# Two more groups of seven products, four groups of query blocks, and rotation tables made once: a change to one inference step of a hybrid decoder layer

## The chip, the cores and the metric

The kernel runs on one core of one Trainium2 chip. The metric is the device time of one execution in microseconds (us), lower is better. Before the change the three timed runs took 1263.16, 1267.95 and 1266.23 us, a median of 1266.23 us.

In the text, PE is the engine for matrix products, PEld its weight loads, DVE the vector engine, ACT the scalar engine, POOL the general engine and SP the engine whose queue issues most of the transfers. L1382 is line 1382 of the kernel before.

## The reference

One layer reads 536 tokens (16 meta tokens, 512 prompt tokens, 8 sample tokens) of width 2048, all float32. One wide product `x @ w_in` feeds two branches, sliding-window attention and a complex diagonal state space (S5), which are gated and merged:

```python
h = jnp.einsum('btd,de->bte', rmsnorm(x, norm_gain), w_in)
q, k, v, z_a, u, z_s, g_a, g_s = jnp.split(h, IN_SPLITS, axis=-1)   # 1024, 256, 256, 1024, 1024, 1024, 2048, 2048 wide
q, k = rope(rmsnorm(q, q_gain), pos), rope(rmsnorm(k, k_gain), pos)
o_attn = sink_attention(q, k, v, window 128, 16 meta keys)
lam_bar = jnp.exp(lam * dt)                                         # 64 groups x 64 complex states
h_t = lam_bar * h_{t-1} + b_bar @ u_t;  y = gelu(Re(c @ h_t) + d * u)
y = y * sigmoid(y @ w_glu + b_glu)
out = x + (sigmoid(g_a) * ((o_attn * silu(z_a)) @ w_attn_out) + sigmoid(g_s) * ((y * silu(z_s)) @ w_ssm_out)) @ w_out
```

The outputs are the new tokens, the key and value windows and the states.

## The kernel before

**Products.** Every weight and every activation is split into a high and a low part, and each product of 128x128 weights with 260 columns (half of the tokens) is three matmuls: high by high, low by high, high by low. A block is 128 output columns for all tokens; over the 2048 inputs it takes 16 x 3 x 2 = 96 matmuls (`mm`, L1157, the matmul itself L1168). The splits are made while the weights stream in (`Stream.piece`, L1004): a transfer on SP's queue, a cast on ACT (L1008), a subtraction on DVE (L1009), two units of 128x1024 for a block.

**Groups.** `Quads` (L1026) and `quad` (L1386) compute two blocks together by a scheme of the Strassen kind: seven products (`product`, L1379, matmul L1382) of 8 x 3 = 24 matmuls in place of eight. Each group needs four raw units, some of them summed on DVE (L1073), seven casts on ACT (L1074) and seven subtractions on DVE (L1075); the weights are made three products ahead (`get(ahead=3)`, L1083). The activations' sums (`tau`) are made beforehand.

**Order of the work.** The 48 gate blocks ("x"), 8 state space inputs ("u") and 12 heads' blocks ("h": 2 of keys, 2 of values, 8 of queries) come in this order: five x blocks while the input is loaded; NA = 4 x blocks; NQ = 15 groups of two x blocks (L1511); then the list ORDER1 (L946), "x" and then u and h in turn, the last five h in a row; then x blocks until all are made (L1676). The GLU's eight half blocks (Y1), the state space's output product (Y2, 16 half blocks, L1719), the attention's output product (A, L1737) and eight groups for `w_out` (L1771) end the kernel.

**Background.** All other work lies in three lanes of generators (`Background`, L952). After every two or four weight tiles of a block (`GRAIN`) and after every product of a group, `bg.step` adds a budget to a credit (at most `cap` is carried over) and runs generator steps until the credit is spent. Each step yields its cost, by the author's own count in us of DVE; `None` ends a lane's turn. With `fair` set the lanes take turns, otherwise the first lane goes first. Lane 0 holds the state space's preparation (`ssm_prep`), the eight state space sets (`ssm(n)`, begun by each u block) and then `attention()`; lane 1 the sets' constants (`ssm_consts`); lane 2 the decoding samples (`samples`).

This order is only where the code writes the work down. A scheduler then orders each engine's queue by its own plan: weights and evacuations have a high priority, and an instruction may be put ahead of its place in the text when the plan finds its inputs ready and its engine free. `issue_after(ins)` (called `later()` in the generators) puts instructions behind `ins` on the engine of `ins`; `bg.last` is a matmul. An engine works through its queue in order and waits at each instruction for its inputs.

**The state space's preparation** (L149) is a chain of some 200 small POOL instructions on 128x32 to 128x704 elements, in the time of the groups. It makes the powers of the rotation, T6 and T11, last (L272 and L275), and a transposed factor (L287). Its result goes to DRAM (L1499) and is read back when the list ORDER1 begins. In each of the eight sets `ssm_consts` builds the rotation table of 66 steps from T6 and T11 with six DVE instructions (L404 to L421). `ssm_block` (L444) multiplies the inputs by the table (L483, L484), scans two stretches of 66 (L503), rotates back (L509 to L513) and forms the outputs.

**The heads.** `heads(i)` (L1325) multiplies a block by the tokens' norm (L1331) into a tile of the name "z", writes it to DRAM twice, the second time with halves exchanged (five transfers on SP's queue), squares it on ACT, and, after each second block, sums the squares by a small matmul (`sums`, L1349). After the last h block `head_norms` (L1361) loads the sums and takes reciprocal roots by a chain of twelve small DVE instructions, first for the keys (rkD), then for the queries (rqD), in four tiles of the name "z", of which there are two buffers. An x block's evacuation (`evac`, L1198) needs such a tile too; a u block's goes to `uf` (L1581). `attention()` (L1587) begins when `normed` is set behind it: it loads keys, values and queries, rotates them (`rope`, L707, with the roots from rkD and rqD), and goes through four key groups. `samples()` begins at the same place. `attended()` (L1658) splits the attention's result for the product A at the end; `bg.drain()` (L1727) puts down whatever background is left before A.

Of the kernel before, what the change touches and what calls it, by code (L numbers as in the profile page):

```python
# [67 lines left out]
def cmul(v, pool, out, a, br, bi, sh, tag):  # L68
# [14 lines left out]
        ("T6", (2, 32, 6)), ("T11", (2, 32, 11)), ("car", (2, 32)))  # L83
NKEPT = sum(int(np.prod(s)) for _, s in KEPT)
# [53 lines left out]
def kept(ap):  # L138

    r, o = {}, 0  # L140
    for nm, sh in KEPT:
# [7 lines left out]
def ssm_prep(nc, K, tmp, psum, dram, R, ident, a_prm, later):  # L149
# [18 lines left out]
    yield 3.0  # L168
# [6 lines left out]
    yield 3.0  # L175
# [33 lines left out]
    yield 3.0  # L209
# [19 lines left out]
    yield 2.5  # L229
# [15 lines left out]
    def powers(tab, z, cnt, tag):  # L245
# [9 lines left out]
        for zp in zs:  # L255
# [6 lines left out]
            yield 1.5  # L262
        norm(tab, (32, cnt), "nt")
        yield 2.0
# [19 lines left out]
    yield 1.0  # L284
    for _ in range(8):
        yield None
# [12 lines left out]
    yield 0.0  # L299

# [22 lines left out]
def ssm_consts(nc, pool, dram, R, D, ub, a_bT, a_bN, a_cT, e32, d_skip, later, free):  # L323
# [41 lines left out]
    nc.sync.dma_start(out=B, in_=a_bT[ub])  # L365
    CL = pool.tile([P, 4, 2, 5, 32], F32, name="CL")
# [37 lines left out]
    tab = pool.tile([P, 2, 4, L], F32, name="tab")  # L404
    x = R["T11"][:, :, ps]
    y = R["T6"][:, :, ps]
    t1 = pool.tile([P, 4, 11, 6], F32, name="rt1", bufs=1)
    t2 = pool.tile([P, 4, 11, 6], F32, name="rt2", bufs=1)
    tv = tab.rearrange("p r a (i j) -> p r a i j", j=6)

    def outer(dst, i, j):
        v.tensor_tensor(out=dst, in0=bc(x[:, i], 3, 6), in1=bc(y[:, j], 2, 11), op=ALU.mult)
    outer(t1, 0, 0)
    outer(t2, 1, 1)
    v.tensor_tensor(out=tv[:, 0].rearrange("p a i j -> p (a i j)"), in0=t1.rearrange("p a i j -> p (a i j)"),
                    in1=t2.rearrange("p a i j -> p (a i j)"), op=ALU.subtract)
    outer(t1, 0, 1)
    outer(t2, 1, 0)
    v.scalar_tensor_tensor(out=tv[:, 1].rearrange("p a i j -> p (a i j)"), in0=t1.rearrange("p a i j -> p (a i j)"),
                           scalar=-1.0, in1=t2.rearrange("p a i j -> p (a i j)"), op0=ALU.mult, op1=ALU.subtract)  # L420
# [6 lines left out]
    yield 2.4  # L427
# [16 lines left out]
def ssm_block(nc, pool, R, D, ub, y_out, later):  # L444
# [27 lines left out]
    yield None  # L472
    for h in range(2):
        p1 = pool.tile([P, 2, 2, NB, L], F32, name="p1", tag="rt1", bufs=1)
        p2 = pool.tile([P, 2, 2, NB, L], F32, name="p2", tag="rt2", bufs=1)
        for i in range(2):
# [3 lines left out]
            for es, b in parts:  # L480
                a = slice(2 * h + es.start, 2 * h + es.stop)
                bi = b[:, :, 0:NC].rearrange("p e (n l) -> p e n l", l=L)
                v.tensor_tensor(out=p1[:, i, es], in0=bi, in1=bc(tab[:, 0, a], 2, NB), op=ALU.mult)  # L483
                v.tensor_tensor(out=p2[:, i, es], in0=bi, in1=bc(tab[:, 1, a], 2, NB), op=ALU.mult)  # L484
                g = slice(4 * ub + a.start, 4 * ub + a.stop)
                v.tensor_tensor(out=R["sst"][:, g, i], in0=R["A0"][:, g, i], in1=b[:, :, NC:140], op=ALU.add)
        wv = w[:, :, 2 * h:2 * h + 2].rearrange("p n a r l -> p r a n l")
        v.tensor_tensor(out=wv[:, 0], in0=p1[:, 0], in1=p2[:, 1], op=ALU.subtract)
        v.tensor_tensor(out=wv[:, 1], in0=p1[:, 1], in1=p2[:, 0], op=ALU.add)
        yield 3.0  # L490
    tre, tim = bc(tab[:, 0], 2, 2), bc(tab[:, 1], 2, 2)
# [14 lines left out]
    for n in range(NB):  # L506
        t1 = pool.tile([P, 4, 2, L], F32, name="rt1", bufs=1)
        t2 = pool.tile([P, 4, 2, L], F32, name="rt2", bufs=1)
        v.tensor_tensor(out=t1, in0=w[:, n], in1=tre, op=ALU.mult)  # L509
        v.tensor_tensor(out=t2, in0=w[:, n], in1=tim, op=ALU.mult)  # L510
        hs = slice(9 + n * L, 9 + n * L + L)
        v.tensor_tensor(out=H[:, :, 0, hs], in0=t1[:, :, 0], in1=t2[:, :, 1], op=ALU.add)
# [576 lines left out]
def trunk(tc, A, O):  # L1089
# [235 lines left out]
    def heads(i):  # L1325
# [16 lines left out]
        def sums():  # L1342
            if "ax" not in S:
                S["ax"] = aux.tile([P, 2, 512], F32, name="aux")
# [605 lines left out]
```

## Time and profile before

| | |
|---|---|
| timed runs, median (lowest to highest) | 1266.23 us (1263.16 to 1267.95) |
| span of the profiled execution, first to last instruction (the page gives no other time of it) | 1262.3 us |
| mean granted clock of PE | 0.997 |
| instructions | 26,537 |
| beginning, five x blocks among it | 0 to about 42 us |
| x blocks one by one (with two of the five) | to 116.1 us |
| fifteen groups | 116.1 to 420.1 us |
| list ORDER1 and x blocks | 420.1 to 828 us |
| GLU and state space's output product | 828 to 1003.8 us |
| attention's output product | 1003.8 to 1096 us |
| groups of `w_out` | 1096 to 1262.3 us |

The profile's page lists each engine's busy time, then the span in 40 slices; a slice is about 31.6 us. Views of the trace give the busy time in chosen stretches, the instructions in order of time, groups of equal instructions, and who waited for whom. "[2.94 <-DVE t L563]" behind an instruction says that its engine stood idle for 2.94 us before it, and which instruction released it by the profile's inference. Matmul durations overlap, since they are pipelined; the distance from one start to the next is what a matmul takes of the span.

### The profile page before, as it was taken

To read this page: it belongs to the slowest core of one execution; us is meant where nothing else is said; L and a number is where in the kernel's file an instruction comes from. 1 tells how busy PE (TensorE), PEld (TensorE's weight loads), DVE (VectorE), ACT (ScalarE), POOL (GpSimd) and SP (SyncE) were. 2 spreads that over 40 slices of the span, in tenths; PEclk is the share of its full clock that TensorE was granted. 3 is DMA by queue.
4 is the path that set the end of the run, shared out by engine and by line. 5 is a ranking of instruction groups with operands and counts; after the bars stand their busy time and mean duration, and the time that the engine had idled before them with its cause. 6 is when DMAs were issued, how large, how long until landed. Compare 5 with 4: busy or idle time off the path is not lost.

```text
span 1262.3 us, 26537 instructions
## 1 busy us (share of the span) xinstructions
PE 1250.9 (99%) x10357; PEld 1227.7 (97%) x10357; DVE 980.6 (78%) x1554; ACT 628.7 (50%) x1344; POOL 266.1 (21%) x437
## 2 busy tenths in 40 slices
PE   9999999999999999999999999999999999999998
PEld 9999999999999999999999999999999999999998
DVE  8687878887778668888897377899887577887875
ACT  8554445444545586556432235567555333344342
POOL 0003999940000033122220123211011000000000
PEclk9999999999999999999999989999999999999999
DMA  8544343443434656555554775777666756555441
GB/s 294 199 160 153 134 143 110 143 150 134 151 126 146 214 172 182 159 165 167 156 159 121 246 211 182 224 240 225 189 214 203 258 174 189 165 192 163 145 139 51
DMA packets 108001, 219.22 MB, mean 174 GB/s; under 512 B 21932, under 2 KB 47492, under 8 KB 107844
## 3 DMA queue, kind: packets, MB, share of 16 engines
q1 hardware_dynamic: 99172, 198.53, 48.5%
q0 software_dynamic: 8704, 19.00, 5.6%
q8 instruction: 81, 1.33, 0.4%
q14 instruction: 44, 0.36, 0.1%
HBM read 181.57 MB, written 36.82 MB: 173 GB/s over the span
## 4 chain that ended last, share of the span: by engine, by line
PE 92%; DVE 3%; DMA 2%; ACT 1%; SPq 1%; issue 0%; DVEq 0%; ACTq 0%
PE mm L1168 45%; PE pr L1382 35%; PE wg L854 2%; PE mm L1255 2%; PE aux L1382 1%; PE aux L1168 1%; PE aux L1255 1%; DVE wlo L1009 1%; PE aux L806 1%; PE aux L805 1%; ACT ct L346 1%; PE tr L526 1%; PE tr L836 1%; PE wg L526 1%; DMA Y<-yD 0%
## 5 line engine op out<-in xcount | busy, mean ns | idle before, releaser
L1075 DVE TENSOR_TENSOR wlo<-raw,whi 128x1024 fp32r<-128x1024 f32 x161 | 198.5, 1253 | 69.6 <-ACT whi L1074 69.0
L1074 ACT CAST whi<-raw 128x1024 fp32r<-128x1024 f32 x161 | 166.4, 1049 | 167.2 <-DVE raw L1073 80.0
L1168 PE MATMUL mm<-xh,whi 128*128 128x260 f32 (+1 forms) x792 | 185.8, 288 | 3.1 <-DVE t L563 2.9
L1008 ACT CAST whi<-raw 128x1024 fp32r<-128x1024 f32 (+3 forms) x128 | 122.3, 965 | 132.3 <-PE mm L1168 85.6
L1168 PE MATMUL mm<-xh,wlo 128*128 128x260 f32 (+1 forms) x792 | 184.4, 287 | 0.0
L1168 PE MATMUL mm<-xl,whi 128*128 128x260 f32 (+1 forms) x792 | 184.1, 286 | 0.0
L1009 DVE TENSOR_TENSOR wlo<-raw,whi 128x1024 fp32r<-128x1024 f32 (+3 forms) x128 | 142.2, 1119 | 46.5 <-ACT whi L1008 45.7
L1382 PE MATMUL pr<-tau,whi 128*128 128x260 f32 x928 | 168.6, 283 | 0.0
L1382 PE MATMUL pr<-cb,whi 128*128 128x260 f32 x848 | 153.0, 283 | 0.0
L1382 PEld LDWEIGHTS pr<-tau,whi 128*128 128x128 f32 x928 | 143.0, 188 | 0.0
L1168 PEld LDWEIGHTS mm<-xh,whi 128*128 128x128 f32 x792 | 132.5, 189 | 5.8 <-ACT KH L747 3.1
L1168 PEld LDWEIGHTS mm<-xl,whi 128*128 128x128 f32 x792 | 133.1, 190 | 0.4 <-issue 0.4
L1168 PEld LDWEIGHTS mm<-xh,wlo 128*128 128x128 f32 x792 | 132.2, 189 | 0.4 <-issue 0.4
L1382 PEld LDWEIGHTS pr<-cb,whi 128*128 128x128 f32 x848 | 130.8, 188 | 0.2 <-ACT z L1416 0.2
L1382 PE MATMUL pr<-tau,wlo 128*128 128x260 f32 x464 | 130.8, 282 | 0.0
L1382 PE MATMUL pr<-cb,wlo 128*128 128x260 f32 x424 | 119.1, 283 | 0.2 <-DVE wlo L1075 0.2
L1073 DVE TENSOR_TENSOR raw<-raw 128x1024 f32<-128x1024 f32 x91 | 113.9, 1252 | 1.6
L1168 PE MATMUL mm<-Y,whi 128*128 128x260 f32 x576 | 105.1, 287 | 0.0
L1382 PE MATMUL pr<-xl,whi 128*128 128x260 f32 x352 | 98.9, 283 | 0.0
L1382 PE MATMUL pr<-xh,wlo 128*128 128x260 f32 x352 | 98.8, 283 | 0.0
L1382 PE MATMUL pr<-xh,whi 128*128 128x260 f32 x352 | 97.1, 283 | 0.0
L1382 PEld LDWEIGHTS pr<-tau,wlo 128*128 128x128 f32 x464 | 87.2, 188 | 0.0
(421 smaller groups left out, 2974.9 us busy)
## 6 DMA issues: line engine op xcount, KB each, us to landing
raw<-in_w SPq DMA_DIRECT2D x202, 512.0 KB, 4.3
gD<-z SPq DMA_DIRECT2D x34, 260.0 KB, 4.3
t<-gD SPq DMA_DIRECT2D x32, 260.0 KB, 3.1
cache<-in_vc POOLq DMA_DIRECT2D x16, 286.0 KB, 3.5
cache<-in_kc POOLq DMA_DIRECT2D x15, 288.0 KB, 4.0
xr<-in_x SPq DMA_DIRECT2D x16, 268.0 KB, 6.5
xg<-in_x SPq DMA_DIRECT2D x8, 536.0 KB, 4.7
sbw<-rawD SPq DMA_DIRECT2D x16, 260.0 KB, 5.1
```

Of the source, the lines that this page charges most:

```text
L346: nc.scalar.activation(out=dst, in_=src, func=AF.Copy, scale=x)
L526: nc.tensor.matmul(o[n], lhsT=D["CL"][:, 2 * e + n, i, 1:5], rhs=H[:, 2 * e + n, i, 0:140], start=False, stop=(i == 1))
L805: nc.tensor.matmul(ps[:, e, 0:272], lhsT=q, rhs=KH[:, k0:k0 + 272], start=True, stop=False)
L854: nc.tensor.matmul(pv[64 * e:64 * e + 64, 0:256], lhsT=V, rhs=pr[:, e::2], start=(i == 0), stop=(i == len(parts) - 1))
L1008: nc.scalar.copy(out=hi, in_=raw)
L1009: self.dve = nc.vector.tensor_tensor(out=lo, in0=raw, in1=hi.bitcast(F32), op=ALU.subtract).ins
L1073: nc.vector.tensor_tensor(out=o, in0=o, in1=i, op=ALU.add)
L1074: nc.scalar.copy(out=hi, in_=t)
L1075: nc.vector.tensor_tensor(out=lo, in0=t, in1=hi.bitcast(F32), op=ALU.subtract)
L1168: m = nc.tensor.matmul(ps[:, c, 0:W], lhsT=wt[:, k], rhs=xo(kt, c), start=f, stop=l)
L1255: nc.tensor.matmul(ps[:, c, 0:260], lhsT=wt[:, kt % 8], rhs=xk(xo, kt, c, 8), start=f, stop=l)
L1382: m = nc.tensor.matmul(bank, lhsT=wt[:, p], rhs=x(p, e), start=first and f and p == 0, stop=l and p == 7, skip_group_check=not first and l ...
```

## The change

The groups become seventeen; four of them (numbers 9 to 12) compute the eight query blocks, so the others hold 26 x blocks where there were 30. ORDER1 is shorter: four x blocks, eight u and the four h of keys and values. The rotation tables of all eight sets are made once, in `ssm_prep`, by DVE, and go to DRAM by SP's queue; each set loads its own. The tables now hold each entry twice (for the real and the imaginary part), and `ssm_block` does with fewer and larger DVE instructions. `head_norms` follows the last h block (n = 3), with a u block behind it. `attention()` sets the background's later parameters and adds `samples()` itself when its turn comes in lane 0, which is when the last set has ended. Some costs of the generators are halved, one row of `None` grows from 8 to 14, and the groups' budget from 0.4 to 0.5 a step.

```diff
@@ ssm_prep
-    yield 3.0
+    yield 1.6
...
-    yield 1.0
-    for _ in range(8):
+    yield 0.5
+    for _ in range(14):
         yield None
     ft = psum.tile([P, 512], F32, name="tr")
...
     R["FD"] = FD
     yield 0.0
+    R["tabD"] = dram.tile([8, P, 16 * L], F32, name="tabD")
+    t = [f.rearrange("p (r a i j) -> p r a i j", r=2, a=4, j=6) for f in (room[:, 0:8 * L], room[:, 8 * L:16 * L])]
+    for ub in range(8):
+        ps = slice(4 * ub, 4 * ub + 4)
+        with later():
+            for r in range(2):
+                for e in range(2):
+                    v_.tensor_tensor(out=t[r][:, e], in0=bc(T11[:, e, ps], 3, 6), in1=bc(T6[:, r, ps], 2, 11), op=ALU.mult)
+            a, b = (f.rearrange("p r a i j -> p r (a i j)") for f in t)
+            v_.tensor_tensor(out=a[:, 0], in0=a[:, 0], in1=b[:, 1], op=ALU.subtract)
+            v_.scalar_tensor_tensor(out=a[:, 1], in0=a[:, 1], scalar=-1.0, in1=b[:, 0], op0=ALU.mult, op1=ALU.subtract)
+            d = R["tabD"][ub].rearrange("p (x r l) -> p x r l", r=2, l=L)
+            for r in range(2):
+                nc.sync.dma_start(out=d[:, :, r], in_=t[0].rearrange("p r a i j -> p (r a) (i j)"))
+        yield 2.4
@@ ssm_consts
+    tab = pool.tile([P, 2, 4, 2, L], F32, name="tab")
+    nc.sync.dma_start(out=tab.rearrange("p i a r l -> p (i a r l)"), in_=R["tabD"][ub])
...
-    outer(t1, 0, 0)
-    outer(t2, 1, 1)
...
-    outer(t1, 0, 1)
-    outer(t2, 1, 0)
...
-    yield 2.4
+    yield 0.0
@@ ssm_block
-    for n in range(NB):
-        t1 = pool.tile([P, 4, 2, L], F32, name="rt1", bufs=1)
-        t2 = pool.tile([P, 4, 2, L], F32, name="rt2", bufs=1)
-        v.tensor_tensor(out=t1, in0=w[:, n], in1=tre, op=ALU.mult)
-        v.tensor_tensor(out=t2, in0=w[:, n], in1=tim, op=ALU.mult)
...
-        yield 2.2
+    for t, i in ((t1, 0), (t2, 1)):
+        v.tensor_tensor(out=t.rearrange("p n a r l -> p n (a r l)"), in0=w.rearrange("p n a r l -> p n (a r l)"),
+                        in1=bc(tab[:, i].rearrange("p a r l -> p (a r l)"), 1, NB), op=ALU.mult)
+    yield 2.5
...
+    v.tensor_tensor(out=hv[:, 0], in0=v1[:, 0], in1=v2[:, 1], op=ALU.add)
+    v.tensor_tensor(out=hv[:, 1], in0=v2[:, 0], in1=v1[:, 1], op=ALU.subtract)
+    yield 1.4
@@ constants
-GBUDGET = 0.4
+GBUDGET = 0.5
...
-NA, NQ = 4, 15
+NA, NQ = 4, 17
+QHEADS = range(9, 13)
...
-ORDER1 = [(k, 0) for k in "xuhuhuhuhuhuhuhuhhhhh"]
+ORDER1 = [(k, 0) for k in "xuhuhuhuhuxuxuxu"]
@@ trunk, heads
-    def heads(i):
+    def heads(i, sb=None):
...
-        sq = ev.tile([P, 2, W], F32, name="t")
+        if i < 4:
+            sq = ev.tile([P, 2, W], F32, name="t")
+        else:
+            o = 16 * L + 520 * (i % 2)
+            sq = halves(flats[1][:, o:o + 520])
@@ trunk, groups
+        if q in QHEADS:
+            out = lambda n: heads(4 + 2 * (q - QHEADS[0]) + n, y[n])
+        else:
+            nx += 2
+            out = lambda n: evac(XORDER[i0 + n], y[n], y[n])
         def step():
             nonlocal nst
             nst += 1
+            if nst == 4:
+                while pend:
+                    with tc.issue_after(bg.last):
+                        pend.pop(0)()
@@ trunk, the list
             heads(n)
-            if n == 11:
-                pend.extend((head_norms, lambda: bg.add(samples(), lane=2), lambda: normed.append(1)))
+            if n == 3:
+                pend.extend((head_norms, lambda: normed.append(1)))
@@ trunk, attention
         while not normed:
             yield None
+        bg.fair, bg.cap = False, 2.0
+        bud[0] = BUDGET2
+        bg.add(samples(), lane=2)
...
-    bg.fair, bg.cap = False, 2.0
-    bud[0] = BUDGET2
     bg.add(attention())
```

The order of the weights in DRAM follows (`_layout`); it is made on the host and is no part of the time. What is computed stays the same.

More of the change, by code (lines that the diff above doesn't have):

```diff
@@ L135, in spots, with kept @@
     return r
-def kept(ap):
+def kept(ap, names=KEPT):
     r, o = {}, 0
-    for nm, sh in KEPT:
+    for nm, sh in names:
         n = int(np.prod(sh))
@@ L1531, in step @@
                     ws.fill(nst - 4)
-        quad(qs, xs, [banks[k] for k in "abcd"], y, lambda n: evac(XORDER[i0 + n], y[n], y[n]), step=step)
+        quad(qs, xs, [banks[k] for k in "abcd"], y, out, step=step)
     prc.__exit__(None, None, None)
```

86 lines of the change are left out of this document (42 added, 44 removed).

## The prediction

> **What bounds the kernel now.** I read the page first: each engine's busy share, the slices of DVE and of the granted clock, and the chain that ended last.
>
> ```profile
> PE 1250.9 (99%) x10357; PEld 1227.7 (97%) x10357; DVE 980.6 (78%) x1554; ACT 628.7 (50%) x1344; POOL 266.1 (21%) x437
> DVE  8687878887778668888897377899887577887875
> PEclk9999999999999999999999989999999999999999
> PE 92%; DVE 3%; DMA 2%; ACT 1%; SPq 1%; issue 0%; DVEq 0%; ACTq 0%
> ```
>
> PE works 99% of the span and the chain is 92% PE, so time goes by fewer matmuls or fewer gaps between them. One slice of the clock (the 24th, 726 to 757 us) is below 9. Then the busy time by stretch: length, PE, PEld, DVE, ACT, POOL with counts, clock, transfers.
>
> ```profile
> 116.10:420.10 304.00, 304.00 (x2531) 304.00 (x2531) 244.30 (x246) 144.87 (x203) 145.10 (x201) 1.00 0.41 138
> 420.10:674.00 253.90, 252.20 (x2134) 246.91 (x2133) 211.31 (x464) 146.68 (x474) 61.10 (x124) 1.00 0.57 171
> 674.00:816.00 142.00, 139.06 (x1137) 134.54 (x1135) 97.14 (x191) 59.12 (x134) 31.60 (x56) 0.98 0.66 199
> 828.00:1003.80 175.80, 175.80 (x1435) 164.63 (x1434) 142.58 (x269) 105.35 (x281) 23.57 (x42) 1.00 0.67 215
> 298.50:318.80 20.30, 20.30 (x172) 20.30 (x171) 15.76 (x17) 9.65 (x14) 0.00 (x0) 1.00 0.36 131
> 217.40:237.70 20.30, 20.30 (x171) 20.30 (x170) 17.40 (x17) 9.57 (x14) 20.30 (x27) 1.00 0.35 121
> ```
>
> The groups run without a gap: 304.0 us for 2531 matmuls, 0.120 us each, 20.27 us a group. The two last rows are one group each, without and with POOL at work: DVE has 4.5 and 2.9 us left. PE stands 1.7 us in 420 to 674 and 2.9 us in 674 to 816. That second gap, in order of time on PE and on DVE, with what DVE waited for and the clock after it:
>
> ```profile
> 738.06 0.40 PE L1168 MATMUL mm<-xh,wlo 128*128 128x260 f32 x2
> 741.40 0.56 PE L1168 MATMUL mm<-xh,whi 128*128 128x260 f32 x1 [2.94 <-DVE t L563]
> 739.76 0.22 DVE L562 TENSOR_TENSOR t<-z 128x65 f32<-128x65 f32 x1
> 740.57 0.68 DVE L1200 TENSOR_TENSOR z<-mm,R 128x520 f32<-128x520 f32 x1
> DVE sbw L724 <- DMA rb<-rkD: 2.3, 2, 1.2
> DVE z L559 <- DMA rkD<-z: 2.3, 1, 2.3
> 741.40:747.38 5.98, 5.98 (x27) 0.50 1.04 257
> 747.38:758.90 11.52, 11.52 (x98) 1.00 0.94 261
> ```
>
> PE needs a bank that the evacuation L1200 frees, and L1200 needs a "z" tile that `head_norms` (L562) holds. That chain is slow since `attention()` has begun beside it: DVE stands in its queue for the key roots that the chain itself makes (L724, L559). The gap costs 2.9 us, and then 27 matmuls take 5.98 us at half clock, which at the next row's 11.52/98 = 0.118 us would take 3.2: 2.8 us more.
>
> **The change part by part.** The sum is made against the span, 1262.3 us; the median of the runs is 1266.2, 3.9 above it, and I take that offset as unchanged.
>
> Groups. Four blocks of 96 matmuls go (384) and two groups of 168 come (336): 48 matmuls less at 0.120 us are **-5.8 us**. Weight work on DVE and ACT moves with them: a group has seven subtractions and four sums where two blocks have four subtractions. DVE has 15.8 of 20.3 us in such a group, so it still fits; without that cover DVE would set the pace.
>
> The gap. `head_norms` now follows h block 3 with a u block behind it, whose evacuation needs no "z" tile, and `attention()` no longer runs beside it. The "z" tile is wanted at the end of the x block after that, one block (11.5 us) later than now, and the evacuation was only 2.9 us late. I take the whole gap and its half clock as gone: **-5.7 us**; the bounds are 0 (another wait takes its place) and -5.7.
>
> By the Trainium skill, TensorE: Matmul & The Clock Gate, section "What's actually happening", the clock halves after an idle window of about 3.4 us and comes back after a busy one. By that length alone a gap of 2.94 us need not halve the clock, 2.8 us would stay, and the sum would come to 1259; the windows run freely, though, and the row shows the half clock right behind this gap, so the row decides.
>
> Tables. Four products and two combinations for each of eight sets move from the sets to the groups.
>
> ```profile
> L412 DVE TENSOR_TENSOR rt<-kept 128x264 f32<-128x264 f32 x32 | 12.3, 425 | 0.1
> L415 DVE TENSOR_TENSOR tab<-rt,rt 128x264 f32<-128x264 f32 x8 | 3.4, 429 | 0.1
> L419 DVE SCALAR_TENSOR_TENSOR tab<-rt,rt 128x264 f32<-128x264 f32 x8 | 3.4, 431 | 0.2
> B<-in_bT SPq DMA_DIRECT2D x8, 512.0 KB, 3.5
> 737.79 2.43 SPq L734 DMA_DIRECT2D out_k<-sbw  x2
> ```
>
> That is 32 x 0.425 + 16 x 0.43 = 20.5 us of DVE. In the groups DVE has 4.5 us to spare once POOL is done, so it takes 4.6 groups, and about nine are left then: 0 us. If the cover is gone, PE loses what exceeds the three products made ahead, 3 x 2.9 = 8.7 us. What the tables wait for is the second rival. On SP's queue come 16 writes of tables (0.3 to 1.2 us of issue each, by the last row's two in 2.43), eight loads of 528 KB (like B's, 3.5 us to land), and the heads' five transfers for each of eight blocks, which move from ORDER1 to the groups. The weights' loads, a block or three products ahead, cover them: 0, at worst one late load of 3.5 us.
>
> Sets. Each loses those 2.6 us of DVE and some fixed cost by the merged instructions; the DVE there was busy 211 of 254 us and PE stood for 1.7 us. Bounds: -1.7 (the waits go) to +1.7 (as much again, since the last set now ends beside attention's beginning). The squares, sums and evacuations of the query blocks are the same instructions elsewhere; the groups' y tiles are free for two groups, 40 us, where their transfers need some 5.
>
> Attention. These rows are DVE's last output of the last set, attention's first copies, the splits for A, and A's first matmul.
>
> ```profile
> L536 DVE SCALAR_TENSOR_TENSOR g<-g,tr x8: 433/438/445, 483.6 to 687.8; 128x280 f32<-128x280 f32 x8
> L762 DVE COPY vb<-sv x4: 274/304/715, 721.4 to 722.6; 128x256 f32<-128x256 f32 x4
> L1656 DVE TENSOR_TENSOR A<-oT,A x8: 691/694/700, 992.3 to 997.3; 128x520 fp32r<-128x520 f32 x8
> 1003.89 0.64 PE L1168 MATMUL mm<-A,whi 128*128 128x260 f32 x4
> ```
>
> Now 33 us lie between the last set and attention; the change takes them out, and four blocks of room with them. I added up the yields by hand: a set costs 23.9 before and 20.8 after, two blocks give 25.6, so the sets keep up with the u blocks. Attention then begins with about 6.2 x blocks left where it was 6.5, and `attended()` ends in the 14th half block of Y2 where it was the 13th. A half block is 175.8 / 24 = 7.3 us; the first split would stand at 999.6 on the old scale, before the first use at 1003.9, and the eight splits keep ahead of A, which uses one every 0.72 us. So 0, with little left: each further half block would cost up to 7. For new waits where attention begins beside the set's last transfers I take **+1.5**, about the 1.7 us of the sets' stretch.
>
> Sum: -5.8 - 5.7 + 1.5 = -10.0: span 1252.3, time **1256.2 us**. A measurement of this kernel can tell about 0.5%, 6.3 us, from no change: faster means below 1259.9, slower above 1272.6.
>
> **The rivals.** First, the groups' gain alone. The gap turns up again where attention now begins, or the background ends a half block later than counted. For it: 33 us of distance are gone, and the margin at A was 6.6 us. Against it: the key roots are long made by then. With one such gap, 5.7 us, it gives about 1262, in all 1260 to 1272: no change.
>
> Second, on the other side: **DVE stands before the first table** until POOL has made T11. POOL's and DVE's instructions at the beginning of the preparation, then POOL's counts in two stretches, a slow instruction and the one that completes T11:
>
> ```profile
> 112.81 0.16 POOL L247 MEMSET work<- 128x32 f32 x1 [111.97 <-PE mm L1168]
> 114.54 1.18 POOL L158 TENSOR_TENSOR work<-work 128x32 f32<-128x32 f32 x1 [1.38 <-DMA work<-in_prm]
> 117.17 0.24 POOL L160 TENSOR_TENSOR work<-work 128x32 f32<-128x32 f32 x1
> 115.54 0.73 DVE L1206 SCALAR_TENSOR_TENSOR z<-t,z 128x520 f32<-128x520 f32 x1
> 117.44 0.35 DVE L165 RECIPROCAL work<-work 128x32 f32<-128x32 f32 x1 [1.17 <-POOL work L160]
> 112.00:187.00 75.00, 68.16 (x109) 1.00 0.40 137
> 187.00:265.60 78.60, 78.05 (x97) 1.00 0.35 117
> 183.88 1.23 POOL L78 TENSOR_TENSOR work<-work 128x32 f32<-128x32 f32 x1
> 259.67 2.17 POOL L243 TENSOR_TENSOR work<-work 128x704 f32<-128x704 f32 x1
> ```
>
> L247 stands far down in the text and ran first; L165 stands seven steps later in the text and was put into DVE's queue so early that DVE waited 1.17 us for POOL. So an instruction of the preparation goes where the plan finds it ready, and `later()` names a PE matmul, which no row shows to hold DVE. The plan can have given POOL's five instructions up to L160 at most 116.27 - 114.54 = 1.73 us, 0.35 each, where the whole chain's 206 took 153.6, 0.75 each (a 128x32 instruction takes 0.24 or 1.2). At 0.35 the plan has the chain ready after 72 us, at 187, when 97 instructions are still to come. With DVE standing, these would run at about 0.35: DVE waits 34 us, PE has 8.7 us of products made, stands 25, and pays 2.8 for the clock: 28 more, **about 1284 us**. Against it: chains whose links wait for each other cost more in a plan than loose instructions, and at the table's place in the text (by my count step 45, 116.1 + 45 x 2.9 = 246) only 15 us of the chain are left, some 7 us of POOL alone, which the 8.7 us cover. So it decides from where the first table stands in DVE's queue: behind about 245 us it costs nothing, and each us earlier, at the plan's pace, about half a us.
>
> **How the numbers follow.** Gain as summed, 1251 to 1260: 0.42. First rival, 1260 to 1272: 0.20. Second, 1272 to 1300 with 1284 as its price: 0.38. The first is the likeliest, so I predict 1256.2; its own range is 1251 (the sets' waits go too) to 1260. The range for 8 in 10 takes the first rival whole and the second up to a little above its price, 1251 to 1286; what lies above, a plan that is earlier still, is about 0.15. The cases give faster 0.42, same 0.20, slower 0.38.
>
> **What would show it.** Seventeen groups should take 17 x 20.27 = 344.6 us without a gap; no half clock between the groups' end and the GLU; no wait of PE for L563. A wait of DVE of more than 9 us for POOL at the first table's product, with PE idle behind it and the clock halved, would show the second rival. The A splits should come one half block nearer to A's first matmul; if PE waits there, the first rival holds. If the groups take clearly more than 20.3 us while DVE is full, the tables or the added transfers were priced too low.

## The result, and the profile after

| kernel | median of the runs, us | profiled execution, us | its span, us | mean granted clock |
| --- | --- | --- | --- | --- |
| before | 1265.8 (1263.2 to 1268.0, 4 runs) | see above | 1262.3 | 0.997 |
| after | 1312.7 (1311.1 to 1314.4, 4 runs) | 1312.2 | 1310.5 | 0.982 |

The kernel became slower: 1.0372 times the time before, interval 1.0354 to 1.0389, 47 us where 10 us less were predicted. The time lies above the predicted range too.

The head of the page of after: engines, the slices of PE and of the granted clock, and the engines' shares of the chain that ended last.

```profile
PE 1255.0 (96%) x10309; PEld 1228.8 (94%) x10309; DVE 986.0 (75%) x1526; ACT 637.3 (49%) x1358; POOL 216.4 (17%) x437
...
PE   9999982989999999999999998999999999999998
...
PEclk9999995999999999999999999999999989999999
...
PE 72%; DMA 8%; POOL 8%; DVE 7%; issue 3%; ACT 1%; SPq 1%; DVEq 0%; ACTq 0%; POOLq 0%
```

PE has its 48 matmuls less (10309 against 10357), but the chain is now 72% PE instead of 92%: POOL, transfers and DVE each hold 7 to 8% of it. One slice of PE, the seventh (197 to 229 us), is nearly empty, and the clock is halved there. POOL, with the same 437 instructions, is busy 216 us instead of 266: for a long while nothing stood beside it.

What PE waited for, from the end of the first stage on: releaser, total us, times, longest.

```profile
PE pr L1395 <- DVE wlo L1079: 33.4, 5, 29.2
PE tr L775 <- DMA sbw<-rawD: 3.4, 1, 3.4
PE mm L1172 <- ACT A L1678: 3.2, 1, 3.2
```

The wait for `head_norms` that cost the kernel before 2.9 us is not among them: that part of the prediction came true. The largest waits are now three others: a weight subtraction of the groups that came 29 us late, the first values of attention, and the split for A. For the first, DVE and PE in order of time:

```profile
179.44 3.70 DVE L1079 TENSOR_TENSOR wlo<-raw,whi 128x1024 fp32r<-128x1024 f32 x3 [0.53 <-ACT whi L1078]
217.87 1.71 DVE L308 TENSOR_TENSOR work<-work 128x264 f32<-128x264 f32 x4 [34.73 <-POOL work L244]
...
191.29 0.28 PE L1395 MATMUL pr<-xl,whi 128*128 128x260 f32 x1
220.77 0.58 PE L1395 MATMUL pr<-xh,wlo 128*128 128x260 f32 x1 [29.21 <-DVE wlo L1079]
```

The first table (L308) stands in DVE's queue behind a subtraction that ended at 183.1. DVE stood there 34.73 us for POOL's T11 (L244). PE went on with the products made ahead until 191.6, 8.4 us, and then stood 29.21. The second rival of the prediction had said 187, 34, 8.7 and 25 us.

The loss by stretch: length, PE, PEld, DVE, ACT, POOL, clock, transfers.

```profile
116.10:232.00 115.90, 85.68 (x686) 85.18 (x685) 69.05 (x79) 38.73 (x53) 98.53 (x201) 0.85 0.32 101
232.00:300.00 68.00, 62.27 (x490) 60.42 (x489) 55.11 (x81) 27.03 (x39) 0.00 (x0) 0.97 0.81 168
300.00:506.00 206.00, 206.00 (x1723) 203.77 (x1722) 158.71 (x169) 99.38 (x142) 0.00 (x0) 1.00 0.46 146
506.00:760.00 254.00, 250.50 (x2114) 245.32 (x2113) 195.56 (x390) 146.19 (x473) 70.79 (x137) 1.00 0.64 183
760.00:874.00 114.00, 107.43 (x875) 105.18 (x874) 88.57 (x168) 50.95 (x114) 22.09 (x45) 0.99 0.76 227
874.00:1060.00 186.00, 182.23 (x1466) 169.66 (x1465) 144.28 (x281) 109.78 (x310) 21.82 (x44) 0.98 0.67 210
```

PE stands 30.2 us in the first stretch, most of it the one stand. In the second, POOL is done and PE still stands 5.7 us, with the transfers at 0.81; the third is free of both. The last two, attention's beginning and end, hold 10.3 us of idle PE and some half clock. So there are three places to ask about: the stand at 190, the stretch from 232 to 300, and attention.

### The profile page after: what moved, and what is told of

Read it like the earlier page. It is cut to its first block, busy times and chain, and to the rows that moved or that the text cites. A ratio compares the mean times of both kernels' runs of the same rounds, so it can differ in the third digit from the quotient of the medians.

```text
span 1310.5 us, 26440 instructions
## 1 busy us (share of the span) xinstructions
PE 1255.0 (96%) x10309; PEld 1228.8 (94%) x10309; DVE 986.0 (75%) x1526; ACT 637.3 (49%) x1358; POOL 216.4 (17%) x437
## 4 chain that ended last, share of the span: by engine, by line
PE 72%; DMA 8%; POOL 8%; DVE 7%; issue 3%; ACT 1%; SPq 1%; DVEq 0%; ACTq 0%; POOLq 0%
PE mm L1172 34%; PE pr L1395 28%; DMA tabD<-work 3%; PE wg L858 2%; PE mm L1259 2%; DMA sbw<-rawD 1%; DVE wlo L1013 1%; PE aux L1172 1%; DMA c<-in_cT 1%; PE aux L1259 1%; POOL work L63 1%; POOL work L62 1%; POOL work L75 1%; POOL work L42 1%; PE aux L809 1%
## 5 line engine op out<-in xcount | busy, mean ns | idle before, releaser
L1078 ACT CAST whi<-raw 128x1024 fp32r<-128x1024 f32 x175 | 180.3, 1048 | 216.4 <-DVE raw L1077 123.5
L1395 PE MATMUL pr<-tau,whi 128*128 128x260 f32 x1056 | 194.9, 286 | 1.7 <-DVE t L1430 1.0
L1395 PEld LDWEIGHTS pr<-tau,whi 128*128 128x128 f32 x1056 | 165.4, 191 | 2.2 <-DVE t L1430 1.3
L1172 PE MATMUL mm<-xh,whi 128*128 128x260 f32 (+1 forms) x696 | 162.9, 287 | 0.2 <-ACT xr L1232 0.2
L1172 PE MATMUL mm<-xh,wlo 128*128 128x260 f32 (+1 forms) x696 | 162.6, 287 | 0.0
L1172 PE MATMUL mm<-xl,whi 128*128 128x260 f32 (+1 forms) x696 | 162.0, 286 | 0.0
L1395 PE MATMUL pr<-tau,wlo 128*128 128x260 f32 x528 | 150.6, 286 | 3.7 <-DVE wlo L1079 3.7
L1172 PEld LDWEIGHTS mm<-xh,whi 128*128 128x128 f32 x696 | 116.2, 189 | 1.2 <-issue 0.6
L1172 PEld LDWEIGHTS mm<-xl,whi 128*128 128x128 f32 x696 | 116.7, 189 | 0.2 <-issue 0.2
L1172 PEld LDWEIGHTS mm<-xh,wlo 128*128 128x128 f32 x696 | 116.0, 189 | 0.7 <-issue 0.6
L1395 PE MATMUL pr<-xh,whi 128*128 128x260 f32 x400 | 112.6, 286 | 1.0 <-ACT whi L1078 0.8
```

The costliest lines, as they stand in the source:

```text
L1078: nc.scalar.copy(out=hi, in_=t)
L1172: m = nc.tensor.matmul(ps[:, c, 0:W], lhsT=wt[:, k], rhs=xo(kt, c), start=f, stop=l)
L1395: m = nc.tensor.matmul(bank, lhsT=wt[:, p], rhs=x(p, e), start=first and f and p == 0, stop=l and p == 7, skip_group_check=not first and l ...
```

## The experiments

Each run was timed beside runs of the kernel before on the same chip, so the ratios are compared; 1% is 12.7 us. Edits are against the kernel after, or against the run that is named.

**Place of the first table.** `later()` names a PE matmul, and the first table stood at 183 us all the same, so it did not hold the table's instructions on DVE. In these two runs the table's DVE instructions are issued behind the newest weight subtraction instead, at the step the text gives them (45), and ten steps later.

```diff
+            self.dve = nc.vector.tensor_tensor(out=lo, in0=t, in1=hi.bitcast(F32), op=ALU.subtract).ins
...
-        with later():
+        with hold():        # tc.issue_after(qs.dve)
...
-    for _ in range(14):
+    for _ in range(24):     # second run only
```

> The tables' six DVE instructions are held behind the newest weight subtraction of the groups at the step where the program makes them (step 45, near 246 us by the plan), so that the first one no longer stands in DVE's queue at 183 us; nothing else differs from the kernel after. Theory (place in DVE's queue): DVE can stand only for what POOL still has to do at 246 us, 7 to 20 us of it at POOL's pace beside DVE and less when DVE stands, which the products made ahead cover in large part. The 29.2 us stand of PE and the half clock behind it go, 33 us of the 46.5: about 1280 us, and 1272 us if the tables, now spread over more groups, also stop waiting for their room's transfers (5.7 us of PE's waits and one half clock between 260 and 300 us). Rival (DVE's load in the groups is too much, wherever the tables stand): PE's waits for weight subtractions come back later in the groups, and the time stays above 1300 us.

> As the run before it, with ten steps more ahead of the tables, some 30 us, so that POOL's chain has ended (265 us in the kernel before) when the first table is due. Theory (place in DVE's queue): no wait of DVE for POOL at all; 1270 to 1275 us, 0 to 8 us under the run before it. Rival (DVE's load): no better than the run before it, or worse, as the tables now also meet the query groups' extra subtractions. In both the gaps at the attention's beginning (3.4 us of PE) and end (3.8 us) stay.

At step 45: 1292.2 us, ratio 1.0199 (1.0172 to 1.0225). At step 55: 1277.4 us, 1.0079 (1.0051 to 1.0106). The sign is the theory's, the sizes are not: about 1280 us was expected at step 45, and 1270 to 1275 us at step 55. DVE's waits for the tables' transfers at step 45, then at step 55, and its wait for POOL at step 45:

```profile
DVE work L308 <- DMA tabD<-work: 15.0, 5, 3.3
```

```profile
DVE work L308 <- DMA tabD<-work: 10.2, 6, 2.9
```

```profile
251.74 1.72 DVE L308 TENSOR_TENSOR work<-work 128x264 f32<-128x264 f32 x4 [8.89 <-POOL work L244]
```

At step 45 the wait for POOL is 8.89 us instead of 34.73; at step 55 there is none. But the waits of the tables for their own transfers, 13.5 us in after, did not go away by spreading the tables over more groups. That is a cost of its own.

**The tables' transfers.** Each table has one room, and leaves it in two transfers that write 264 B pieces side by side in memory; the next table's first product waits until both have landed. In the next run, with the tables at step 55, a table leaves in one piece of 2112 B a partition; with that go two more differences, loads of half the size in the sets and four products a block instead of two.

```diff
-            d = R["tabD"][ub].rearrange("p (x r l) -> p x r l", r=2, l=L)
-            for r in range(2):
-                nc.sync.dma_start(out=d[:, :, r], in_=t[0].rearrange("p r a i j -> p (r a) (i j)"))
+            nc.sync.dma_start(out=R["tabD"][ub], in_=room[:, 0:8 * L])
...
-    tab = pool.tile([P, 2, 4, 2, L], F32, name="tab")
+    tab = pool.tile([P, 2, 4, L], F32, name="tab")
...
+        for n in range(NB):     # four products a block instead of two
+            v.tensor_tensor(out=t[:, n], in0=w[:, n], in1=bc(tab[:, i], 2, 2), op=ALU.mult)
```

> The run with ten steps more, but each table leaves in one transfer of 2112 B a partition instead of two of 264 B pieces, is loaded undoubled, and the blocks multiply in four instructions instead of two, as the run with the tables in the sets does. What it shows is what the transfers of pieces cost. Theory (the pieces hold the one room and the queues): DVE's wait of 10.2 us for the tables' transfers falls under 4 us and PE's waits between 250 and 420 us nearly go; 1270 to 1274 us, near the run with the tables in the sets. Rival (the transfers are hidden, the tables cost by DVE's time in the groups or by the sets' earlier start): 1276 to 1279 us.

1267.4 us, ratio 1.0014 (1.0001 to 1.0028): 8 us under the run with pieces by the ratios, more than expected. Four of them lie in the groups, where only the writes differ (352.5 us for the seventeen groups with pieces, 348.4 us here); what the smaller loads and the four products do behind the groups was not tried alone. DVE's wait for these transfers over the whole run is 0.2 us:

```profile
  DMA tabD<-work: 0.2, 1
```

Two more runs put the whole writes beside the two earlier places of the first table: with nothing held, as in after, and held at step 45.

> The kernel after with its tables written whole and loaded undoubled, and nothing held: the first table stands in DVE's queue behind the same three weight subtractions as in the kernel after. Theory (the stand for POOL and the transfers of pieces are two costs that add): the first stand is back whole, DVE waiting some 35 us and PE 29 us at 190 to 221 us with its half clock, while the later waits of DVE for the tables' transfers (13.5 us in the kernel after) are gone: 10 to 12 us under the kernel after, 1300 to 1303 us. Rival (the two overlap, and the 10 us by which the whole write helped at step 55 came from the transfers' load on the queues there): 1308 us or more.

> The kernel after with its tables written whole, and the first table held at its own step (45), where the prediction priced it at nothing: some 7 us of POOL's work alone, covered by 8.7 us of products made ahead. Theory (as the prediction had it for that place): DVE waits 8 to 9 us for POOL, PE hardly, and the time is that of the run with ten steps more and whole writes, 1267 us, or up to 3 above it. Rival (the cover is less than 8.7 us once the groups' own queue has no slack): PE waits 4 to 6 us behind DVE's wait, with a half clock, and the time is 1273 to 1277 us.

Nothing held: 1300.1 us, 1.0289 (1.0269 to 1.0309), as its theory had it. Step 45: 1274.5 us, 1.0077 (1.0060 to 1.0094), in the range of its rival. DVE's waits in the groups, nothing held:

```profile
DVE work L308 <- POOL work L244: 34.8, 1, 34.8
```

and the transfers of tables between 218 and 300 us, after first, then this run (packets of all transfers; then count, KB each, median us from issue to landing):

```profile
DMA packets 19297, 12.78 MB, mean 156 GB/s; under 512 B 16667, under 2 KB 16923, under 8 KB 19291
...
tabD<-work SPq DMA_DIRECT2D x16, 264.0 KB, 6.4
```

```profile
DMA packets 4418, 11.61 MB, mean 142 GB/s; under 512 B 480, under 2 KB 736, under 8 KB 4411
...
tabD<-work SPq DMA_DIRECT2D x8, 264.0 KB, 3.1
```

The stand is as long as in after, and the time is 10.5 us less by the ratios: two costs. They don't add exactly, since the whole writes bring 15 us at step 45 and 8 at step 55. DVE's wait for the tables' transfers falls from 13.5 to 2.0 us, while the weights' own loads in this stretch land as before (median 5.1 us in after, 5.0 here); so it is mainly the wait for the room, and not a late weight, that the pieces cost. A transfer of the same 264 KB lands in 3.1 us instead of 6.4 when it is not cut into pieces, and half as many are needed. The Trainium skill, DMA: Bandwidth & Descriptors, section "Specifications", says that below 512 B a transfer no longer runs at full rate; the 16667 small packets against 480 and the two landing times agree with it.

At step 45 the prediction had priced the wait at nothing. DVE of that run:

```profile
239.82 2.73 DVE L1077 TENSOR_TENSOR wlo<-raw,whi 128x1024 fp32r<-128x1024 f32 x2
251.43 1.73 DVE L308 TENSOR_TENSOR work<-work 128x264 f32<-128x264 f32 x4 [8.87 <-POOL work L244]
253.07 1.21 DVE L1077 TENSOR_TENSOR wlo<-raw,whi 128x1024 fp32r<-128x1024 f32 x1
254.21 0.42 DVE L311 SCALAR_TENSOR_TENSOR work<-work 128x264 f32<-128x264 f32 x1
254.55 0.42 DVE L310 TENSOR_TENSOR work<-work 128x264 f32<-128x264 f32 x1
254.90 1.21 DVE L1077 TENSOR_TENSOR wlo<-raw,whi 128x1024 fp32r<-128x1024 f32 x1
```

and PE:

```profile
256.16 0.39 PE L1393 MATMUL pr<-xh,wlo 128*128 128x260 f32 x1 [3.40 <-DVE wlo L1077]
```

The wait itself was covered: PE ran on until 252.8, 1.3 us past the end of it. But when DVE came back it had the first table's six instructions and two subtractions to do before PE's next weights were there, 4.7 us. PE stood 3.40 for them, and paid the half clock. The cover has to hold the wait and what stands in the queue between it and the next useful instruction. The groups take 354.6 us here and 348.4 at step 55, so 6 of the 8 us between the two runs lie in them; behind them PE's wait for attention's first query is longer too, 7.3 us for 4.5.

**The tables back in the sets.** Each set makes its table with six DVE instructions, as the kernel before; everything else stays as in after.

```diff
-        ("car", (2, 32)))
-MADE = KEPT + (("T6", (2, 32, 6)), ("T11", (2, 32, 11)))
+        ("T6", (2, 32, 6)), ("T11", (2, 32, 11)), ("car", (2, 32)))
...
-    tab = pool.tile([P, 2, 4, 2, L], F32, name="tab")
-    nc.sync.dma_start(out=tab.rearrange("p i a r l -> p (i a r l)"), in_=R["tabD"][ub])
+    tab = pool.tile([P, 2, 4, L], F32, name="tab")
+    outer(o1, 0, 0)
...
```

> The tables part undone: each set makes its own table with six DVE instructions as the kernel before does, no table goes through memory, and each block multiplies in four instructions instead of two; the query groups, the order of the state space and the attention's new beginning stay. Theory: the groups hold no stand and no transfer wait, 389.9 us minus about 41, and what is left of the loss lies behind them: 1268 to 1275 us. Rival (the query blocks in the groups cost more than they bring, or the merged blocks): the groups still show waits, and the time stays over 1280 us. If instead the time is at or under 1262 us, the losses behind the groups came from the tables' transfers too.

1269.9 us, ratio 1.0027 (1.0014 to 1.0040), as the theory had it. The groups' first and last weight loads, after first, then this run (minimum, median, maximum in ns; then the starts in us):

```profile
L1395 PEld LDWEIGHTS pr<-tau,whi x1056: 186/188/338, 116.1 to 505.7; 128*128 128x128 f32 x176
```

```profile
L1391 PEld LDWEIGHTS pr<-tau,whi x1056: 187/188/195, 116.7 to 464.9; 128*128 128x128 f32 x176
```

Without the tables the seventeen groups take 348 us: the 344.6 of the prediction and the 32 short matmuls of the query heads' sums, which now lie among them. With them they took 389.6. So the tables as they were written cost 41 us in the groups (44 us of the whole time by the ratios), and the query blocks in the groups are sound. The same length, from the groups' first to their last weight load, for each run:

| tables | groups, us | ratio |
| --- | --- | --- |
| in pieces, nothing held (after) | 389.6 | 1.0372 |
| written whole, nothing held | 380.9 | 1.0289 |
| in pieces, step 45 | 368.4 | 1.0199 |
| written whole, step 45 | 354.6 | 1.0077 |
| in pieces, step 55 | 352.5 | 1.0079 |
| written whole, step 55 | 348.4 | 1.0014 |
| in the sets | 348.2 | 1.0027 |

Tables in the groups done well take no more of the groups than no tables at all. Their time (1.0014) and that of the tables in the sets (1.0027) have overlapping intervals: moving them showed no gain beyond a microsecond or two.

**Attention's beginning and end.** What is left in that run, as PE's waits:

```profile
PE aux L805 <- DVE QT L789: 5.4, 1, 5.4
PE mm L1168 <- ACT A L1674: 3.2, 1, 3.2
```

Two gaps: the first scores stand for the first query, and A's first matmul for the split. Three runs moved steps of the background's plan against them. The first has the tables at step 55, in pieces, and three steps more between attention's first loads and their use:

```diff
-        yield None
+        for _ in range(4):
+            yield None
```

> The run with ten steps more, and three steps more between the loads of attention's first tiles and their first use. Theory (the attention starts before its loads have landed): the 3.4 us gap of PE at the transposes of the values goes with its half clock, 5 us; by the planner's arithmetic the attention then also ends two half blocks earlier, so that the wait for the attention's split (3.8 us of PE, 6.8 us of half clock, about 7 us) goes too: 1258 to 1265 us. Rival: the gap moves to the next load (keys), and the end stays where it was: no difference from the run with ten steps alone.

1273.8 us, 1.0056 (1.0033 to 1.0080): 3 us less by the ratios than without the three steps, with intervals that overlap, and far from the 1258 to 1265 us of the theory. The waits for the first values and for A went. PE's wait for the first queries stayed, 5.9 us, and two new ones came, of 2.1 and 1.6 us. The second run takes the tables in the sets, the same three steps, `NLOAD` 7 for 3, and `BUDGET3, BUDGET4` 3.8 and 5.2 for 3.4 and 4.8:

> The run with the tables in the sets, and the attention's ends mended: three steps more between the loads of its first tiles and their use, seven steps instead of three ahead of its first queries, and larger budgets of the background work in the last two stages (3.8 and 5.2 instead of 3.4 and 4.8), so that by the planner's arithmetic it ends a half block earlier. Theory (what is left of the loss in that run is PE waiting 5.4 us for the first queries and 4.2 us for the attention's split, each with a half clock behind it): both go, 10 us and 2 to 5 us of clock, 1255 to 1260 us, under the kernel before. Rival (the gaps only move, since DVE has no room between 740 and 880 us): 1265 to 1270 us, with new waits of PE of 3 us or more in the same stretch or at the end.

1267.4 us, 1.0020 (1.0008 to 1.0031), 1 us under the run with the tables in the sets, within both intervals. The third takes the tables written whole at step 55, one step, `NLOAD` 5, `NDELAY` 3 for 1, and the same budgets:

> The run with tables written whole, and the attention's ends mended in another way than before: one step more between the first loads and their use, two more between the queries' loads and the queries, two more between the first queries and the first scores, and larger budgets of the background work in the last two stages (3.8 and 5.2 instead of 3.4 and 4.8), by which the planner's arithmetic has the attention's split a half block earlier although it begins its scores later. Theory (what is left in that run is PE's wait of 4.5 us for the first queries and of 3.7 us for the split, with a half clock behind each): both go, 8 us and 2 to 5 us of clock: 1255 to 1260 us, faster than the kernel before by more than 0.4%. Rival (DVE and the transfer queues are full between 740 and 880 us, so that a gap closed at one place opens at another): 1264 to 1268 us with PE's waits of 5 us or more in sum behind 740 us.

1269.0 us, 1.0035 (1.0023 to 1.0048), rather worse than without these edits (1.0014). The theory failed both times. The times are those of the rival in the second run, and 1 us above them in the third: PE's wait for the first queries shrank to 3.4 and 2.1 us, and a new one opened 65 to 75 us later, 2.0 and 2.6 us. In the third run:

```profile
PE mm L1170 <- ACT A L1677: 4.5, 1, 4.5
PE mm L1170 <- ACT t L1734: 2.6, 1, 2.6
PE aux L807 <- DVE QT L791: 2.1, 2, 1.5
```

The split came no earlier although by the author's count the plan had moved it by half a block. DVE, PE and POOL in that run show what it hangs on:

```profile
996.09 0.60 PE L856 MATMUL wg<-pp,V 128*64 128x256 f32 x4
...
998.81 1.79 POOL L915 DMA_DIRECT2D zs<-gD  x2 [33.03 <-issue]
...
1001.64 0.18 DVE L926 SCALAR_TENSOR_TENSOR oT<-aux,zs 64x32 f32<-64x32 f32 x1 [4.42 <-DMA zs<-gD]
...
1003.82 4.32 ACT L1677 CAST A<-oT 128x520 fp32r<-128x520 f32 x8 [2.96 <-DVE oT L926]
```

The gates `zs` of the last rows share a room (`dV`) with the last block's product. Their load can't start until PE has read it, lands 2.8 us later, and only then DVE, and then the split, go on: 7 us of chain behind the last product, wherever the plan puts it. In the first of the three runs the chain is there as well, and PE did not wait, since its last product ended 8 us earlier than without the three steps (999.7 us for 1007.6). The first queries hang on a room too: their load needs an "sbw" tile that the keys' rotation still holds. In the run with whole writes it is issued at 759.6 us, when the last instruction of that rotation (758.9 us, 0.7 long) ends. The last three runs take away these two dependences instead of moving steps, on top of the tables written whole at step 55; each has the edit of the one before.

```diff
-        zs = pool.tile([P, 8, 2, 4], F32, name="zs", tag="dV", bufs=1)
+        zs = pool.tile([P, 8, 2, 4], F32, name="zs", bufs=1)
...
+        if i == 4:              # second and third run
+            sb, sw = (pool.tile([P, 2, W], F32, name="q0", tag="sv") for _ in range(2))
...
-        yield None              # third run
+        for _ in range(2):
+            yield None
```

> The run with tables written whole, and the eight-row gates of the attention's end (zs) in a tile of their own instead of the room that the last block's product reads, so that their transfer no longer starts only behind that product (998.4 us there, 2.8 us to land). Theory (the attention's split is late by that chain, not by the planner's step): PE's waits of 3.2 and 0.5 us for the split go, and the half clock behind them: 5 to 7 us less than the run with tables written whole, 1261 to 1263 us. Rival (DVE's queue or the planner's step holds the split): unchanged, 1266 to 1268 us.

> As the run before it, and the first query is loaded into the two small rooms that the values have left, instead of the room that the keys' rotation still holds, with no step moved. Theory (the first scores wait for a load that waits for the keys' room): the 4.5 us wait of PE for the first queries goes with its half clock, 6 to 7 us: 1254 to 1257 us, under the kernel before by 0.6 to 0.9%. Rival (the transfer queue is full there, DMA share 0.80): the load lands no earlier, 1260 to 1263 us.

> As the run before it, with one step more between the loads of the attention's first tiles and their use. Theory: PE's wait of 1.1 us for the first values goes as well, 1 us less or no difference from the run before it. Rival (a step more at the beginning makes the end late): 1 to 4 us more, with PE waiting for the split.

1266.0 us, 1.0005 (0.9996 to 1.0014); 1266.3 us, 1.0004 (0.9992 to 1.0016); 1262.8 us, 0.9975 (0.9964 to 0.9985). PE's waits from 640 to 1040 us in the second and in the third run:

```profile
PE aux L810 <- DVE QT L794: 2.9, 2, 1.6
PE wg L859 <- ACT pm L847: 1.8, 1, 1.8
PE wg L859 <- DVE po L845: 1.7, 2, 1.2
```

```profile
PE aux L810 <- DVE QT L794: 2.3, 2, 1.2
PE wg L859 <- ACT pm L847: 2.1, 1, 2.1
PE mm L1173 <- DVE z L1205: 1.7, 1, 1.7
PE aux L810 <- DVE S L816: 1.3, 2, 0.9
```

As the theory said of the dependences, the wait for A's split is gone from the first of these runs on. With its own room the first query's load is issued at 753.7 us, 6 us earlier, and PE's wait for the query, 4.5 us in one piece without the edits, is 2.9 and 2.3 us in two pieces each. The times did not follow: 5 to 7 us and then 6 to 7 us were expected, and 1 and 0 came, since other waits of 1 to 3 us opened at other instructions of the same blocks. From 640 to 1040 us PE stands 10.6 us without the edits, 9.3 and 9.7 in the first two runs, and 7.4 in the third. That run is faster than both kernels, than the one before by 0.25%, 3 us. It is less than the 0.5% that the prediction took for a difference, but the interval does not hold 1. It also gained more than the 1 us of its theory; the traces, one execution each, do not show why: the profiled execution of the second run took 1263.7 us, 2.6 us under its median, so its view shows less waiting than most of its executions can have had.

## Why the prediction was wrong, point by point

- **Groups, -5.8: right.** 48 matmuls went, and the groups without the tables' stands take what the sum said (348 us with the sums).
- **The gap at `head_norms`, -5.7: right as to the wait.** No run of the changed kernel has a wait of PE for it. The 2.8 us of half clock in the term were those of one profiled execution: 5.98 us at half clock take about 0.24% off the mean (an estimate from the span), and some executions of the kernel before have a mean clock of 1.000.
- **Tables, "0 us": the step that failed**, in three places. First, the likeliest case put the first table at step 45, although the same text showed by L247 and L165 that the plan puts such instructions where it finds them ready; the second rival, held back to 0.38, was what happened, with its row, its length and its cause right and its price short: 28 us, where the groups with whole writes are 32.5 us longer with nothing held than at step 55 (380.9 for 348.4), most of it since PE stood 29 us and not 25. From nothing held to step 45 the ratio falls by 2.1%, 27 us. Second, "only some 7 us of POOL alone, which the 8.7 us cover": 8.9 us at step 45, itself covered, and still the groups are 6 us longer than at step 55 (354.6 against 348.4), because the six table instructions and two subtractions stood behind the wait. Third, the 16 writes were priced by their issue on SP alone. That the next table needs the room they leave was not seen: 0.8% or 10.5 us with nothing held. The price of DVE's own work in the groups, 0 us, was right: at step 55 and written whole, the tables take nothing of the groups.
- **Attention's beginning, +1.5: mis-sized.** In the run with whole writes at step 55, PE stands 5.7 us between 760 and 874 us at a clock of 0.97 (about 3 us more), most of it for the first query. The prediction looked at the instructions beside it and not at the rooms that the first loads need.
- **Attention's end, 0: mis-sized.** PE stands 3.7 us between 874 and 1040 us at 0.98 (about 3 us). The prediction moved the splits by one half block, 7.3 us; by that the first, a cast at 991.6 us before, would stand 5 us ahead of A's first matmul (1003.9). In this run it stands 2.5 us behind the place where PE arrives at A (1002.7 against 1000.2). The 7.5 us between the two are about the chain through `zs`, 7 us, which the prediction did not have. That was the first rival's second half. With the tables repaired, 1267.4 us lies in what that rival gave, 1260 to 1272.
- **Sets, -1.7 to +1.7:** PE stood 3.5 us between 506 and 760 us in after, where it stood 1.7 before: the upper bound.
- **The offset, 3.9 us:** part of it was chance. In the executions on record the time is 1.7 to 1.8 us above the span, so the profiled execution before took about 1264.1 us, 2.1 less than the median. It changes nothing of the outcome.

The rows of that run behind the two attention terms:

```profile
760.00:874.00 114.00, 108.31 (x875) 104.22 (x875) 100.58 (x184) 65.89 (x166) 19.53 (x37) 0.97 0.80 245
874.00:1040.00 166.00, 162.26 (x1305) 151.91 (x1302) 119.88 (x220) 88.19 (x238) 14.25 (x30) 0.98 0.63 196
```

```profile
PE aux L807 <- DVE QT L791: 4.5, 1, 4.5
PE mm L1170 <- ACT A L1676: 3.2, 1, 3.2
```

With these sizes the sum for the run with whole writes at step 55 is -5.8 - 5.7 + 8.7 + 6.7 = +3.9 us; measured were 0.14%, 1.8 us.

The two mistakes differ. The attention terms were mis-sized. The tables' place was a choice between two readings of one's own evidence: rows of this very kernel showed an instruction of the preparation in DVE's queue far ahead of its place in the text, and against them stood only a count of the text. That the range ended at 1286 was a second consequence: the rival was taken "up to a little above its price", without what else would go wrong beside it; in the run the stand, the rooms and attention's ends added up.

## What to carry to other kernels

An instruction that waits for a slow engine must be tied to something on its own engine, or a scheduler that places by readiness may put it where its estimate of that engine is most wrong; a dependence on another engine's instruction held nothing here. A moved step brings its rooms along: ask of each tile that it writes or loads who must let go of it and how long the letting go takes, for a write to memory until it has landed. When gaps wander as steps of a plan are moved, look for the room or the load that the late instruction really hangs on, and take that away.

## What the runs showed of the hardware

A gap need not be 3.4 us to halve the clock. In after, one of 2.77 us did. PE, then the stretches behind it (length, PE with count, clock, transfers):

```profile
276.92 0.58 PE L1395 MATMUL pr<-tau,wlo 128*128 128x260 f32 x1 [2.77 <-DVE wlo L1079]
```

```profile
276.92:278.50 1.58, 1.58 (x7) 0.50 1.11 215
...
280.40:284.00 3.60, 3.60 (x33) 1.00 0.90 204
```

Seven matmuls in 1.58 us are 0.226 each, twice the 0.109 of the second row. By the Trainium skill, TensorE: Matmul & The Clock Gate, section "What's actually happening", the idle window is about 3.4 us. Here shorter gaps halved the clock too: 2.94 us in the kernel before, 2.34 us in the run with whole writes and nothing held (0.50 from 784.2 to 787.2 us), 2.10 us in the last run (0.50 from 852.6 to 854.6 us). Others as long did not: 2.10 us at 867.9 us in the first run with steps moved, 2.58 us at 851.1 us in the third, with a clock of 1.00 over the 4 us behind each. So the length of one gap does not decide it, and what else does no run here shows. The mean clock of the kernel before lay between 0.997 and 1.000 over its executions, so a half clock in one profile need not be in the next execution.

POOL's speed depends on what DVE does far more than its own work would tell: the same 437 instructions were busy 266.1 us before and 216.4 in after, where DVE stood beside them for 35 us. In that stand, from 183.1 to 217.8 us, 105 of them took 34.2 us, 0.33 each; the last 97 of the preparation before, beside a busy DVE, took 78.1 us, 0.80 each. So a stand of DVE for POOL is shorter than POOL's remaining time as read beside a busy DVE.
